# Ones-tile products in two groups (25 and 5), a sixth VectorE row in the first modulation block, and square passes of the second token block's statistics placed later

## The chip, the core and the metric

The kernel runs on one core of one Trainium2 chip. A core has engines that each work through their own list of instructions: TensorE (PE in the profile, with its weight loads as PEld), VectorE (DVE), ScalarE (ACT), GpSimd (POOL) and SyncE (SP), which here issues most DMA transfers. They wait for each other through semaphores. On-chip memory is SBUF; matmul results go to eight PSUM banks of 128 x 512 fp32. The metric is device time of one launch in microseconds (us), smaller is better.

## The reference

One decoder layer on x (4096 tokens x 1024), conditioned by one vector c. `layer_norm` is over the last axis, without affine parameters.

```python
mod = jax.nn.silu(c) @ w_ada + b_ada
shift, scale, gate = jnp.split(mod, 3, axis=-1)
h = layer_norm(x) * (1.0 + scale[:, None, :]) + shift[:, None, :]
proj = h @ w_in + b_in
u_a, z_a, glu_b, z_b = proj[..., :o1], proj[..., o1:o2], proj[..., o2:o3], proj[..., o3:]
pooled = causal_multiscale_pool(u_a)              # windows 2, 4, 8, 16, less the token itself
y_a = jnp.einsum("bsgc,gcd->bsgd", pooled, w_pool) + b_pool
y_a = y_a.reshape(y_a.shape[0], y_a.shape[1], D_POOL) * ls_pool * jax.nn.silu(z_a)
v = glu_b[..., :D_CONV] * jax.nn.sigmoid(glu_b[..., D_CONV:])
v = causal_depthwise_conv(v, w_dw, b_dw)          # 31 taps, 512 channels
v = jax.nn.silu(layer_norm(v) * ln_conv_g + ln_conv_b)
y_b = (v @ w_pw + b_pw) * jax.nn.silu(z_b)
y = jnp.concatenate([y_a, y_b], axis=-1) @ w_out + b_out
x = layer_norm(DEEPNORM_ALPHA * x + gate[:, None, :] * y) * ln_post_g + ln_post_b
```

## The kernel before

**Tiling.** The 4096 tokens are eight blocks of 512 (`NSB`, `T`), each of four tiles of 128 tokens (`TT`); the 1024 features are eight chunks of 128 (`KT`). For the projections a block lies turned, features on the partitions, tokens along the row. Each fp32 operand is split into a high part that TensorE takes as fp32r and a low remainder, and a product of two is three matmuls: high times high (L370), high weight times low x (L371), low weight times high x (L372). `W[n]` are the 20 column groups of `w_in`; groups 8 to 15 (weights `wg0` to `wg7`, one tile for each feature chunk) feed the GLU, 16 and 17 the first half of `z_b` (weights `wz0`, `wz1`).

**Start: modulation and the first block, chunk by chunk.** `c` and the vectors are loaded and turned by small PE transposes (`cps`, `vpsa`). Then PE runs `WARM` = 18 products of a 128 x 128 tile of ones into a bank of their own; nothing reads them. Shift and scale come in five blocks of feature chunks (`mods`). A block's sum over the eight rows k of `w_ada` is divided: the first `MOD_ROWS[b]` rows are added up on DVE (`macc`, L195, or on ACT for the first row of the wide blocks), the others are PE products with a one-column operand (L209), and a last product with the ones tile adds up DVE's share over the partitions. `MOD_SPREAD` deals DVE's rows of the later blocks over the chunks of the first token block. That block is loaded token-wise, normalised (`stats_dve`, ACT), turned on PE (`turn_x`), and `mod_turned` applies scale and shift: ACT writes the high part (L354) and `hs` (L356), DVE the low part. For each chunk k, PE runs six banks (column groups 8, 12, 9, 13, 10, 14) through three groups of six products (L493, then L497, then L501), with the next chunk's transposes between. Four of the banks are of the ring `acc`, two of the ring `s2`; transposes and modulation use the ring `tp` of two. The upper quarter of `wg` comes late, in two loads `w3r` (`w3_cols`, L458), after chunks 5 and 6.

**Statistics of the second block.** Its four token-wise tiles `x_early` are loaded with the last `w_ada` tiles. `col_stats` takes a sum pass over a tile on ACT (L293), the mean on DVE (L294), a square pass on ACT (L298), the variance on DVE (L299) and the reciprocal root on POOL (L300). When all four tiles are done, `to_rows` turns the eight columns on PE, ACT copies them out (`rowsx`, L306), a DMA writes them to DRAM (`rD`) and another reads them back spread over all partitions (`xbc`, L317).

**Later blocks.** `norm_T` loads two turned chunks of x (`xk`, L324), adds the mean (L325) and multiplies by scale and root (L327) on DVE; `mod_xT` adds the shift on ACT and forms the low part on DVE (L337). Column groups 8 to 15 of a block (`glus`) give the banks `p`; `glu` takes a sigmoid on ACT (`sg`, L521) and one DVE pass (`v`, L523), stored to DRAM (`vD`, L524). `z_half` is two more banks (`p1z`). From the third block on statistics are taken in the same way, without early tiles. A second pass then reloads the turned blocks for groups 0 to 7 and the pooling mixer. Beside all of it DVE computes the depthwise convolution (`conv`: loads `cv`, taps L663 and L665, results `ca`), whose results PE turns (L77) for their layer norm. The last stage is the pointwise product, the output projection (`po`, L802) and the post norm.

**What sets the order.** Three engines follow a hand-written order at the start: `seq(engine, inst)` ties an instruction behind the last one that `seq` placed on that engine (`tails[engine]`), without a semaphore. Everything else is placed by the scheduler of the framework, which simulates a timeline and, on each engine, takes what is ready first, by the order of the program. For the statistics of the second block `leads` holds, for each of its four tiles, the tails of ACT and DVE as they stand after chunk 4, 4, 5 and 6: a tile's sum pass and mean come behind them, its square pass and variance wherever the scheduler puts them.

Of the kernel before, what the change touches and what calls it, by code (L numbers as in the profile page):

```python
# [12 lines left out]
AF = mybir.ActivationFunctionType  # L13
ALU = mybir.AluOpType
# [15 lines left out]
WINDOWS = (2, 4, 8, 16)  # L30
UH = 8
EPS = 1e-5
MOD_ROWS = (5, 6, 7, 8, 8)
MOD_SPREAD = ((2, 7), (0, 6), (1, 3), (0, 4), (0, 3), (0, 3))
BLOCKS = ((0, 1), (1, 2), (3, 2), (5, 1))
EARLY = 2
WARM = 18
GATE_SB = 2
PERSB = (1, 1, 1, 1, 1, 1, 0, 0)
ALPHA = 2.0 ** 0.25  # L40
# [3 lines left out]
def tile_layer(ctx, tc, x, x_t, w_in_t, c, w_ada, b_ada, w_in, b_in, w_pool, b_pool, ls_pool, w_dw, b_dw,  # L44
# [81 lines left out]
        nc.vector.tensor_copy(cols[:, c0 : c0 + r0], vps[:, :r0])  # L126

    load_cols((("b_ada", b_ada, 24), ("b_in", b_in, 20)), nc.scalar.dma_start, "a")
    warm = tp_bank("warm")
    for _ in range(WARM):  # L130
        seq("pe", nc.tensor.matmul(warm[:, :P], ones, ones, start=True, stop=True))
# [159 lines left out]
    def col_stats(src, n, nmean, rstd, name, lead=None):  # L291
        sm = st.tile([P, 3], F32, tag=f"sm{name[0]}", bufs=4, name=f"sm{name}")
        i = nc.scalar.activation(src, src, AF.Identity, accum_out=sm[:, 0:1])  # L293
        mean = nc.vector.tensor_scalar(nmean, sm[:, 0:1], -1.0 / n, None, op0=ALU.mult)  # L294
        if lead is not None:
            after(i, lead[0])
            after(mean, lead[1])
        nc.scalar.activation(src, src, AF.Square, bias=nmean, accum_out=sm[:, 1:2])  # L298
        nc.vector.tensor_scalar(sm[:, 2:3], sm[:, 1:2], 1.0 / n, EPS, op0=ALU.mult, op1=ALU.add)  # L299
        nc.gpsimd.tensor_tensor(rstd, sm[:, 2:3], mhalf[:, 0:1], op=ALU.pow)  # L300

    def to_rows(pb, cs, dst, name):
# [6 lines left out]
    def row_stats(sb):  # L309
        cs = st.tile([P, 8], F32, tag="cs", bufs=2, name=f"xcs{sb}")  # L310
        for t in range(TT):
            i = sb * TT + t
            xt = x_early[t] if sb == 1 else load_x(i, t % 2)
            col_stats(xt, D, cs[:, t : t + 1], cs[:, 4 + t : 5 + t], f"x{i}", leads[t] if sb == 1 else None)
        to_rows(tp_bank(f"xcp{sb}"), cs, rD[sb], f"x{sb}")
        bc = ph.tile([P, 2, T], F32, tag="tm", bufs=5, name=f"xbc{sb}")
        nc.sync.dma_start(bc, rD[sb].rearrange("(a t) p -> a (t p)", a=2).partition_broadcast(P))  # L317
        return bc
# [165 lines left out]
    for k in range(KT):  # L484
        lo = both(Wg[k][1])[:, :, : 3 * P]
        seq("dve", nc.vector.tensor_tensor(lo, rows[k], whi.bitcast(F32), op=ALU.subtract))
        sums(k, 0)
        xT.append(mod_turned(pb, k))
        sums(k, 1)
        if k + 1 < KT:  # L490
            whi = cast_w(k + 1)
        for n0, ps in zip(first, pss0):
            seq("pe", nc.tensor.matmul(ps, W[n0][k][0], xT[k][0], start=k == 0, stop=False))  # L493
        if k + 1 < KT:
            pb = turn_x(xt_next, k + 1)
        for n0, ps in zip(first, pss0):
            seq("pe", nc.tensor.matmul(ps, W[n0][k][0], xT[k][1], start=False, stop=False))  # L497
        if k + 1 in starts:
            closers[starts[k + 1]]()
        for n0, ps in zip(first, pss0):  # L500
            seq("pe", nc.tensor.matmul(ps, W[n0][k][1], xT[k][0], start=False, stop=k == KT - 1))  # L501
# [393 lines left out]
```

## Time and profile before

| | |
|---|---|
| median of 3 runs | 1384.91 us (1384.74 to 1386.92) |
| profiled execution, its own time | 1383.35 us |
| its span, first to last instruction | 1381.4 us |
| mean granted TensorE clock | 0.993 |
| HBM read, written | 156.65 MB, 86.04 MB |
| DMA | 243.83 MB, mean 177 GB/s |

The page's second part cuts the span into 40 slices of 34.5 us and gives the busy share of each in tenths, with the clock that the throttle granted to TensorE:

```
PE   7999999999999999999999999999999999999997
DVE  5769999999999889999869998668796999997754
PEclk8999999999999999999999999999999999999999
```

The start is the first two slices. A timeline row names start, length, engine, source line, operation, written tile <- read tiles, their shapes and how many instructions the row holds; brackets give the idle time before it and what ended it. `SPq` is SP's DMA issue, and a `DMA` row is the transfer itself. Tile names in the trace stand without their numbers, so `xk` is `xk_0`, `xk_2` and so on. One product of the program can be several records of PE.

### The profile page before, as it was taken

What the parts mean: (1) busy time and instruction counts of PE and PEld (TensorE: products, weight loads), DVE (VectorE), ACT (ScalarE), POOL (GpSimd) and SP (SyncE); (2) the same over time, 40 slices, a digit from 0 to 9 for tenths busy, and PEclk for the clock granted to TensorE, in tenths of its full rate; (3) what the DMA queues carried; (4) which work ended last, traced back from release to release, by engine and by line L of the source; (5) the groups of instructions that cost most, each with busy time, mean ns of one, the idle gap of its engine ahead of it and who ended that gap; (6) DMA issues with size and microseconds to landing.
All of it is one profiled execution on the core that took longest, in us unless ns stands there. A gap on an engine that the chain in (4) does not pass through costs nothing.

```text
span 1381.4 us, 17276 instructions
## 1 busy us (share of the span) xinstructions
PE 1361.7 (99%) x6109; PEld 1124.7 (81%) x6109; DVE 1188.5 (86%) x2339; ACT 434.1 (31%) x775; POOL 139.4 (10%) x193
## 2 busy tenths in 40 slices
PE   7999999999999999999999999999999999999997
PEld 6788888888888888888888888888888888888886
DVE  5769999999999889999869998668796999997754
ACT  3745654532322341111321123323224131223310
POOL 1001110100000221011110120000111111102101
PEclk8999999999999999999999999999999999999999
DMA  9797857565375586052461535435334434334511
GB/s 313 238 343 274 290 215 271 201 236 198 126 263 191 190 251 218 35 184 76 154 205 64 168 123 191 168 115 177 143 130 158 146 131 161 124 128 135 185 61 76
DMA packets 116552, 243.83 MB, mean 177 GB/s; under 512 B 15154, under 2 KB 49778, under 8 KB 116466
## 3 DMA queue, kind: packets, MB, share of 16 engines
q1 hardware_dynamic: 107184, 209.15, 43.7%
q0 software_dynamic: 9216, 33.56, 7.3%
q8 instruction: 48, 0.79, 0.2%
q14 instruction: 38, 0.31, 0.1%
q10 hardware_dynamic: 66, 0.02, 0.0%
HBM read 156.65 MB, written 86.04 MB: 176 GB/s over the span
## 4 chain that ended last, share of the span: by engine, by line
PE 82%; DVE 9%; DMA 5%; ACT 1%; issue 1%; SPq 1%; DVEq 0%; ACTq 0%
PE po L802 25%; PE p L370 4%; PE p L371 4%; PE p2z L370 4%; PE p2z L371 4%; PE p2u L372 4%; PE p2u L371 4%; PE p2z L372 4%; PE p2u L370 4%; PE p L372 4%; DVE ca L665 2%; PE pw L780 2%; PE pw L779 2%; PE pw L778 2%; PE p2b L371 2%; PE p2b L372 2%
## 5 line engine op out<-in xcount | busy, mean ns | idle before, releaser
L665 DVE SCALAR_TENSOR_TENSOR cx<-cv,wdw,cx 128x257 f32<-128x257 f32 (+1 forms) x240 | 143.0, 607 | 0.2
L665 DVE SCALAR_TENSOR_TENSOR ca<-cx,wsum,ca 128x256 f32<-128x256 f32 (+1 forms) x240 | 142.3, 607 | 0.0
L665 DVE SCALAR_TENSOR_TENSOR ca<-cv,wdw,ca 128x256 f32<-128x256 f32 (+1 forms) x224 | 133.2, 607 | 0.0
L831 POOL TENSOR_TENSOR ors<-ove,mhalf 128x1 f32<-128x1 f32 x32 | 47.9, 1497 | 421.8 <-DVE ove L827 413.4
L825 ACT ACTIVATE ojk<-r,osm 128x1024 bf16<-128x1024 f32 x31 | 35.7, 1151 | 151.5 <-DVE osm L822 151.5
L365 POOL DMA_DIRECT2D x2r<-xD x64 | 34.5, 539 | 467.9 <-PE p2b L372 287.0
L820 DVE SCALAR_TENSOR_TENSOR r<-po,r 128x512 f32<-128x512 f32 x62 | 40.7, 682 | 30.6 <-PE po L802 30.6
L665 DVE SCALAR_TENSOR_TENSOR lx<-lv,wdw,lx 128x257 f32<-128x257 f32 x120 | 57.3, 477 | 0.0
L665 DVE SCALAR_TENSOR_TENSOR la<-lx,wsum,la 128x256 f32<-128x256 f32 x120 | 57.1, 476 | 0.0
L665 DVE SCALAR_TENSOR_TENSOR la<-lv,wdw,la 128x256 f32<-128x256 f32 x112 | 52.5, 477 | 0.1
L300 POOL TENSOR_TENSOR xcs<-smx,mhalf 128x1 f32<-128x1 f32 x28 | 24.0, 859 | 239.1 <-DVE smx L299 206.4
L293 ACT ACTIVATE x<-x 128x1024 f32<-128x1024 f32 x28 | 29.6, 1058 | 57.4 <-DMA x<-in_x_dram 57.1
L336 ACT ACTIVATE x<-xk,shc 128x512 fp32r<-128x512 f32 x56 | 38.0, 721 | 25.3 <-DVE xk L327 23.1
L595 ACT ACTIVATE sz<-p2z,cols 128x512 f32<-128x512 f32 x32 | 22.0, 687 | 73.3 <-PE p2z L372 69.0
L834 DVE SCALAR_TENSOR_TENSOR r<-r,ors,b_bc 128x1024 f32<-128x1024 f32 (+1 forms) x33 | 41.0, 1244 | 2.7 <-POOL ors L831 2.6
L337 DVE SCALAR_TENSOR_TENSOR x<-xk,shc,x 128x512 fp32r<-128x512 f32 x56 | 40.6, 740 | 2.4 <-ACT x L336 2.4
L794 DVE SCALAR_TENSOR_TENSOR r<-r,gbo 128x1024 f32<-128x1024 f32 x32 | 38.9, 1215 | 3.7 <-DMA r<-in_x_dram 3.7
L759 ACT ACTIVATE t<-t,cols 128x512 f32<-128x512 f32 x32 | 23.1, 724 | 60.1 <-DMA t<-tD 52.1
L219 ACT CAST yb<-z 128x512 fp32r<-128x512 f32 x32 | 19.8, 617 | 68.4 <-DVE z L785 58.4
L802 PE MATMUL po<-wo1h,ya 128*128 128x512 f32 x128 | 41.1, 391 | 0.0
L802 PE MATMUL po<-wo0h,ya 128*128 128x512 f32 x128 | 41.0, 390 | 0.0
L602 ACT ACTIVATE u<-p2u,bu 128x512 f32<-128x512 f32 x32 | 22.0, 687 | 59.0 <-PE p2u L372 58.9
(429 smaller groups left out, 4129.7 us busy)
## 6 DMA issues: line engine op xcount, KB each, us to landing
x2r<-xD POOLq DMA_DIRECT2D x64, 512.0 KB, 7.3
xD<-x SPq DMA_DIRECT2D x56, 512.0 KB
x<-in_x_dram SPq DMA_DIRECT2D x32, 512.0 KB
r<-in_x_dram SPq DMA_DIRECT2D x32, 512.0 KB
out_dram<-r SPq DMA_DIRECT2D x31, 512.0 KB
xk<-in_x_t_dram SPq DMA_DIRECT2D x28, 512.0 KB
wa<-in_w_ada_dram SPq DMA_DIRECT2D x32, 256.0 KB
vD<-v SPq DMA_DIRECT2D x32, 256.0 KB
```

What stands on the lines that cost most here:

```text
L336: nc.scalar.activation(h2[:, 0, :], z, AF.Identity, bias=shc[:, k : k + 1])
L337: nc.vector.scalar_tensor_tensor(h2[:, 1, :], z, shc[:, k : k + 1], h2[:, 0, :].bitcast(F32), op0=ALU.add, op1=ALU.subtract)
L370: nc.tensor.matmul(ps, w[0], X[0], start=first, stop=False)
L371: nc.tensor.matmul(ps, w[0], X[1], start=False, stop=False)
L372: nc.tensor.matmul(ps, w[1], X[0], start=False, stop=last)
L665: nc.vector.scalar_tensor_tensor(dst, src, wt, dst, op0=ALU.mult, op1=ALU.add)
L794: xg = nc.vector.scalar_tensor_tensor(r, r, ALPHA, gbo, op0=ALU.mult, op1=ALU.add)
L802: mm = nc.tensor.matmul(po[h], lhs, Wo[k][wi][:, h * 512 : (h + 1) * 512], start=(k == 0 and wi == 0 and lhs is yh), stop=last)
L820: nc.vector.scalar_tensor_tensor(r[:, sl], po[h], 1.0, r[:, sl], op0=ALU.mult, op1=ALU.add, accum_out=sm[:, h : h + 1])
L825: nc.scalar.activation(jk, r, AF.Square, bias=sm[:, 2:3], accum_out=ss)
L831: nc.gpsimd.tensor_tensor(rs, ve, mhalf[:, 0:1], op=ALU.pow)
L834: nc.vector.scalar_tensor_tensor(r[:, sl], r[:, sl], rs, b_bc[:, sl], op0=ALU.mult, op1=ALU.add)
```

## The change

It edits four places:

- `MOD_ROWS[0]` goes from 5 to 6: in the first modulation block DVE adds up six rows and PE multiplies two, in place of five and three.
- The 18 products of the ones tile become a function `keep_warm(i)`, which writes to a bank of the ring `s2` in place of `tp`. It is called for 25 products at the old place and for 5 more behind the transposes of chunk 0 (`turn_x(xt_next, 0)`), ahead of that chunk's first products.
- `leads` becomes `ends`, the tails of ACT and DVE after every chunk. `X_STATS` names two chunks for each tile of the second block: sum pass and mean go behind the first one's tails (4, 4, 5, 6, as before), square pass and variance now behind the second one's (5, 7, 7, 7).
- In `col_stats` the four instructions of sum and square are tied in one loop.

From the second edit on all lines move down: what was L293, L298, L306, L317, L324, L325, L337, L370, L521 and L665 is L297, L299, L310, L321, L328, L329, L341, L374, L526 and L670.

```diff
@@ -30,11 +30,12 @@
 WINDOWS = (2, 4, 8, 16)
 UH = 8
 EPS = 1e-5
-MOD_ROWS = (5, 6, 7, 8, 8)
+MOD_ROWS = (6, 6, 7, 8, 8)
 MOD_SPREAD = ((2, 7), (0, 6), (1, 3), (0, 4), (0, 3), (0, 3))
 BLOCKS = ((0, 1), (1, 2), (3, 2), (5, 1))
 EARLY = 2
-WARM = 18
+X_STATS = ((4, 5), (4, 7), (5, 7), (6, 7))
+WARM = (25, 5)
 GATE_SB = 2
 PERSB = (1, 1, 1, 1, 1, 1, 0, 0)
 ALPHA = 2.0 ** 0.25
@@ -126,9 +127,12 @@
         nc.vector.tensor_copy(cols[:, c0 : c0 + r0], vps[:, :r0])
 
     load_cols((("b_ada", b_ada, 24), ("b_in", b_in, 20)), nc.scalar.dma_start, "a")
-    warm = tp_bank("warm")
-    for _ in range(WARM):
-        seq("pe", nc.tensor.matmul(warm[:, :P], ones, ones, start=True, stop=True))
+    def keep_warm(i):
+        ps = s2_bank(f"warm{i}")
+        for _ in range(WARM[i]):
+            seq("pe", nc.tensor.matmul(ps[:, :P], ones, ones, start=True, stop=True))
+
+    keep_warm(0)
     wdw = cst.tile([P, CW * MC], F32, name="wdw")
     wsum = cst.tile([P, HQ + 1, MC], F32, name="wsum")
     wd3 = wdw.rearrange("p (j m) -> p j m", m=MC)
@@ -292,11 +296,11 @@
         sm = st.tile([P, 3], F32, tag=f"sm{name[0]}", bufs=4, name=f"sm{name}")
         i = nc.scalar.activation(src, src, AF.Identity, accum_out=sm[:, 0:1])
         mean = nc.vector.tensor_scalar(nmean, sm[:, 0:1], -1.0 / n, None, op0=ALU.mult)
+        sq = nc.scalar.activation(src, src, AF.Square, bias=nmean, accum_out=sm[:, 1:2])
+        var = nc.vector.tensor_scalar(sm[:, 2:3], sm[:, 1:2], 1.0 / n, EPS, op0=ALU.mult, op1=ALU.add)
         if lead is not None:
-            after(i, lead[0])
-            after(mean, lead[1])
-        nc.scalar.activation(src, src, AF.Square, bias=nmean, accum_out=sm[:, 1:2])
-        nc.vector.tensor_scalar(sm[:, 2:3], sm[:, 1:2], 1.0 / n, EPS, op0=ALU.mult, op1=ALU.add)
+            for inst, (act, dve), eng in ((i, lead[0], 0), (mean, lead[0], 1), (sq, lead[1], 0), (var, lead[1], 1)):
+                after(inst, (act, dve)[eng])
         nc.gpsimd.tensor_tensor(rstd, sm[:, 2:3], mhalf[:, 0:1], op=ALU.pow)
 
     def to_rows(pb, cs, dst, name):
@@ -311,7 +315,7 @@
         for t in range(TT):
             i = sb * TT + t
             xt = x_early[t] if sb == 1 else load_x(i, t % 2)
-            col_stats(xt, D, cs[:, t : t + 1], cs[:, 4 + t : 5 + t], f"x{i}", leads[t] if sb == 1 else None)
+            col_stats(xt, D, cs[:, t : t + 1], cs[:, 4 + t : 5 + t], f"x{i}", [ends[k] for k in X_STATS[t]] if sb == 1 else None)
         to_rows(tp_bank(f"xcp{sb}"), cs, rD[sb], f"x{sb}")
         bc = ph.tile([P, 2, T], F32, tag="tm", bufs=5, name=f"xbc{sb}")
         nc.sync.dma_start(bc, rD[sb].rearrange("(a t) p -> a (t p)", a=2).partition_broadcast(P))
@@ -447,7 +451,7 @@
     first = (8, 12, 9, 13, 10, 14)
     pss0 = [acc_bank(f"p1_0_{n0}") for n0 in first[:4]] + [s2_bank(f"p1_0_{n0}") for n0 in first[4:]]
     starts = {k0: b for b, (k0, nk) in enumerate(mods)}
-    leads = []
+    ends = []
 
     def w3_cols(q):
         raw = wraw(f"w3r{q}").rearrange("p (k h c) -> p k h c", k=4, h=2)
@@ -475,6 +479,7 @@
     closers[0]()
     whi = cast_w(0)
     pb = turn_x(xt_next, 0)
+    keep_warm(1)
 
     def sums(k, part):
         if k < len(MOD_SPREAD):
@@ -499,7 +504,7 @@
             closers[starts[k + 1]]()
         for n0, ps in zip(first, pss0):
             seq("pe", nc.tensor.matmul(ps, W[n0][k][1], xT[k][0], start=False, stop=k == KT - 1))
-        leads += [(tails["act"], tails["dve"])] * (0, 0, 0, 0, 2, 1, 1, 0)[k]
+        ends.append((tails["act"], tails["dve"]))
         if k in (5, 6):
             w3_cols(k - 5)
     assert not steps
```

The scheduler's order follows these ties, and it moves more than the four places name. In the rows below, numbers behind a tile's name are the framework's count (`x_446` and `x_449` are the second block's token-wise tiles), and a row's end is the shape.

**ACT, end of the first block** (chunk 7 to the first `sg`). Before, `x_446` is the last of the four tiles (the square passes of the other three stand further ahead, `x_444` two rows ahead of it), `hs_7` the last step of the chunk, and `x_1096` a tile of the third block:

```order
L298 ACTIVATE x_446,smx_888<-x_446,xcs_869 128x1024
L356 ACTIVATE hs_7_792<-x_0_7_790,shn 128x512
L219 CAST wz0h<-wzr_857 128x1024
L219 CAST wz1h<-wzr_863 128x1024
L306 COPY rowsx_896<-xcp_894 8x128
L521 ACTIVATE sg_0_911<-p_0_12_453,cols 128x512
L521 ACTIVATE sg_1_916<-p_0_13_455,cols 128x512
L521 ACTIVATE sg_2_921<-p_0_14_457,cols 128x512
L293 ACTIVATE x_1096,smx_1098<-x_1096 128x1024
```

The same stretch of the change:

```order
L360 ACTIVATE hs_7_804<-x_0_7_802,shn 128x512
L223 CAST wz0h<-wzr_869 128x1024
L299 ACTIVATE x_449,smx_888<-x_449,xcs_881 128x1024
L299 ACTIVATE x_451,smx_894<-x_451,xcs_881 128x1024
L299 ACTIVATE x_453,smx_900<-x_453,xcs_881 128x1024
L223 CAST wz1h<-wzr_875 128x1024
L526 ACTIVATE sg_0_923<-p_0_12_460,cols 128x512
L526 ACTIVATE sg_1_928<-p_0_13_462,cols 128x512
L297 ACTIVATE x_1108,smx_1110<-x_1108 128x1024
L310 COPY rowsx_908<-xcp_906 8x128
L526 ACTIVATE sg_2_933<-p_0_14_464,cols 128x512
```

Three square passes have gone from ahead of `hs_7` to between the two casts of `wz`, and `rowsx` has gone from ahead of the first sigmoid to behind the second and a sum pass of the third block.

**SP's queue, same place.** It issues the statistics' way through DRAM (`rD`, `xbc`), the `xk` loads, the third block's tiles (`x_...<-in_x_dram`) and the GLU's stores (`vD`). Before:

```order
L307 DMA rD_289<-rowsx_896 8x128
L288 DMA x_1096<-in_x_dram 128x1024
L288 DMA x_1104<-in_x_dram 128x1024
L317 DMA xbc_899<-rD_289 128x1024
L324 DMA xk_0_901<-in_x_t_dram 128x2x512
L324 DMA xk_2_906<-in_x_t_dram 128x2x512
L524 DMA vD_0_184<-v_0_913 128x512
```

And of the change, where `cv_0` is the first load of the convolution:

```order
L292 DMA x_1116<-in_x_dram 128x1024
L529 DMA vD_0_191<-v_0_925 128x512
L311 DMA rD_296<-rowsx_908 8x128
L529 DMA vD_0_199<-v_1_930 128x512
L292 DMA x_1124<-in_x_dram 128x1024
L659 DMA cv_0_6493<-vD_0_191 128x2x256
L321 DMA xbc_911<-rD_296 128x1024
L328 DMA xk_0_913<-in_x_t_dram 128x2x512
L328 DMA xk_2_918<-in_x_t_dram 128x2x512
```

Two GLU stores, the third tile of the third block and `cv_0` now stand ahead of `xbc`.

**DVE, norm of the second block**, from the first pass over `xk_0` to the low part of its first chunk, `x_1_0`. Before:

```order
L325 TENSOR_TENSOR xk_0_901<-xk_0_901,xbc_899 128x1024
L299 TENSOR_SCALAR smx_1106<-smx_1106 128x1
L327 SCALAR_TENSOR_TENSOR xk_0_901<-xk_0_901,s_300,xbc_899 128x512 x2
L325 TENSOR_TENSOR xk_2_906<-xk_2_906,xbc_899 128x1024
L523 SCALAR_TENSOR_TENSOR v_2_923<-p_0_10_456,cols,sg_2_921 128x512
L337 SCALAR_TENSOR_TENSOR x_1_0_981<-xk_0_901,shc,x_1_0_981 128x512
```

Of the change, from two rows behind its first pass over `xk_0` (twelve more rows, taps of the convolution and statistics of the third block, stand right ahead of that pass) to the same row:

```order
L670 SCALAR_TENSOR_TENSOR ca_0_6494<-cv_0_6493,wdw,ca_0_6494 128x256
L670 SCALAR_TENSOR_TENSOR ca_0_6494<-cx_0_6495,wsum,ca_0_6494 128x256
L329 TENSOR_TENSOR xk_2_918<-xk_2_918,xbc_911 128x1024
L528 SCALAR_TENSOR_TENSOR v_3_990<-p_0_11_938,cols,sg_3_988 128x512
L331 SCALAR_TENSOR_TENSOR xk_0_913<-xk_0_913,s_307,xbc_911 128x512 x2
L670 SCALAR_TENSOR_TENSOR cx_0_6495<-cv_0_6493,wdw,cx_0_6495 128x257
L670 SCALAR_TENSOR_TENSOR ca_0_6494<-cv_0_6493,wdw,ca_0_6494 128x256
L670 SCALAR_TENSOR_TENSOR ca_0_6494<-cx_0_6495,wsum,ca_0_6494 128x256
L329 TENSOR_TENSOR xk_4_1009<-xk_4_1009,xbc_911 128x1024
L331 SCALAR_TENSOR_TENSOR xk_2_918<-xk_2_918,s_307,xbc_911 128x512 x2
L329 TENSOR_TENSOR xk_6_1014<-xk_6_1014,xbc_911 128x1024
L341 SCALAR_TENSOR_TENSOR x_1_0_993<-xk_0_913,shc,x_1_0_993 128x512
```

Taps of the convolution and the passes over `xk_2`, `xk_4` and `xk_6` now stand between the first pass over `xk_0` and `x_1_0`; on PE the second block's first products wait for `x_1_0`, and begin with three high ones (`p_1_8`, `p_1_12`, `p_1_9`, L374) where one stood before.

## The prediction

> **What bounds the kernel now.** I read the page first, then the chain of waits, then busy time by stretch, then each engine's timeline up to 115 us.
>
> ```profile
> PE 1361.7 (99%) x6109; PEld 1124.7 (81%) x6109; DVE 1188.5 (86%) x2339; ACT 434.1 (31%) x775; POOL 139.4 (10%) x193
> PE 82%; DVE 9%; DMA 5%; ACT 1%; issue 1%; SPq 1%; DVEq 0%; ACTq 0%
> 100.00:160.00 60.00, 60.00 (x267) 49.50 (x266) 54.59 (x133) 32.20 (x53) 7.01 (x8) 1.00 0.79 292
> 260.00:360.00 100.00, 100.00 (x462) 83.12 (x462) 98.47 (x159) 36.10 (x60) 5.88 (x7) 1.00 0.57 204
> ```
>
> The first two rows are engine busy times and the shares of the chain; the other two are stretches (length, then PE, PEld, DVE, ACT, POOL busy, then the granted clock). PE is the bound: from 70 us on it has no gap worth naming, so the end is the moment at which PE's unbroken run begins plus a fixed amount of products. A microsecond won or lost before 70 us, or a new hole in the run, moves the end one for one. DVE is close behind (54.59 of 60 us), so a change in DVE's order can open such a hole.
>
> ```profile
> 0.84 0.17 DVE L70 MEMSET ones<- 128x128 f32 x1 [0.84 <-PEq L878]
> 5.82 6.92 PE L131 MATMUL warm<-ones 128*128 128x128 f32 x36
> 14.29 0.96 PE L209 MATMUL mod<-sc,wa 128*128 128x1 f32 x6 [1.55 <-DMA wa<-in_w_ada_dram]
> 13.84 1.01 DVE L195 SCALAR_TENSOR_TENSOR macc<-wa,sc,macc 128x256 f32<-128x256 f32 x2
> 19.21 2.93 PE L493 MATMUL p<-x,wg0h 128*128 128x512 f32 x6 [0.87 <-ACT x L354]
> 35.52 2.76 PE L493 MATMUL p<-x,wg2h 128*128 128x512 f32 x6
> 41.60 1.53 PE L493 MATMUL p<-x,wg3h 128*128 128x512 f32 x6
> 15.00:18.00 3.00, 3.00 (x16) 2.94 (x15) 0.54 (x4) 1.48 (x2) 0.00 (x0) 0.50 1.18 305
> 36.00:38.00 2.00, 2.00 (x6) 1.50 (x5) 1.97 (x4) 0.69 (x1) 0.00 (x0) 0.50 1.10 347
> 57.00:60.00 3.00, 1.15 (x6) 0.61 (x5) 2.40 (x9) 2.97 (x7) 0.55 (x1) 1.00 0.01 3
> ```
>
> Timeline rows read start, length, engine, line, output<-input, count, and in brackets the wait before and its releaser. The granted clock is 0.50 in 15 to 18 us and again in 36 to 38: six products take 2.76 us there and 1.53 at full clock.
>
> **The products and the sixth row: no effect on the end.** Two records make one product, so 18 products take 6.92 us, 0.38 each. Twenty-five take 9.6 us; from 1.0 us, when `ones` is set, with two small transposes between, they are over near 11.2, and the wait for w_ada still ends at 14.29. The gap ahead of it grows from 1.55 to about 3 us, and after 1.55 the clock was already at 0.50, so I expect it there again. In the first modulation block PE loses two of eight products (four records of 0.16 us, 0.64 us) and DVE gains one row of 0.5 us, which the first summing product then waits for by some 0.3: net 0.3 us earlier. The five products take 1.9 us where PE waited 0.87: up to 1.0 us later. An unbroken run may lift the clock sooner, and six half-clock products cost 1.2 us more. So PE reaches the second modulation block between 1.5 us earlier and 1 us later. What hides it:
>
> ```profile
> 53.67 0.41 ACT L458 CAST wg0h<-w3r 128x256 fp32r<-128x256 f32 x1 [0.73 <-DMA w3r<-in_w_in_dram]
> 57.45 1.13 ACT L298 ACTIVATE x<-x,xcs 128x1024 f32<-128x1024 f32 x1
> 58.58 0.76 ACT L354 ACTIVATE x<-xt,shc,s 128x512 fp32r<-128x512 f32 x1
> 59.39 1.68 PE L493 MATMUL p<-x,wg6h 128*128 128x512 f32 x6 [1.85 <-ACT x L354]
> 65.93 0.71 ACT L356 ACTIVATE hs<-x,shn 128x512 f32<-128x512 f32 x1
> 66.54 1.03 ACT L219 CAST wz0h<-wzr 128x1024 fp32r<-128x1024 f32 x1
> 68.89 0.25 ACT L306 COPY rowsx<-xcp 8x128 f32<-8x128 f32 x1
> 69.63 1.27 ACT L521 ACTIVATE sg<-p,cols 128x512 f32<-128x512 f32 x2 [0.49 <-PE p L501]
> 70.37 0.50 PE L370 MATMUL p<-x,wg0h 128*128 128x512 f32 x1
> ```
>
> At 59.39 PE has waited 1.85 us for ACT, and ACT's work there hangs on a load that lands at 53.67 whatever PE did. A gain before lengthens that wait, a loss of under 1.85 us shortens it. I take 0; were the cover gone, the ends above would count in full.
>
> **The square passes: PE's run begins 1.2 us earlier.** After the casts at 53.67 ACT ran one sum and two squares (1.13 us each) ahead of chunk 6; now one, so chunk 6 starts 1.13 us earlier, near 58.3. Of the four squares, three stood ahead of `hs_7` after 57 us; 3 x 1.13 = 3.4 us off 66.54 lets ACT be done with `hs_7` at 63.1. PE then has the block's last product done near 67.7 instead of 70.37. But ACT now runs the first cast of wz (0.95 us), three squares (3.4), the second cast (0.96) and `sg_0` (0.64) in a row: 69.1. `p_0_11`, the first product of the unbroken run, needs the bank that `sg_0` reads (before, too, it followed it by 0.1). So it starts at 69.2 against 70.37: 1.2 us gained, between 0.5 and 1.6, as casts and loads fall. The transpose of the statistics needs the last square, 67.5, plus about 1 us over DVE and POOL: earlier than 69.2.
>
> **The statistics' way to the second block: late.** `rowsx`, the copy that sends the statistics on, now stands behind `sg_0`, `sg_1` and a sum pass for the third block: 69.7 plus 1.14 plus 0.2 is 71.05, against 69.14.
>
> ```profile
> 69.82 0.33 SPq L307 DMA_DIRECT2D rD<-rowsx  x1
> 73.35 0.33 SPq L317 DMA_DIRECT2D xbc<-rD  x1
> 73.72 0.94 SPq L324 DMA_DIRECT2D xk<-in_x_t_dram  x2
> 76.43 1.06 ACT L293 ACTIVATE x<-x 128x1024 f32<-128x1024 f32 x1 [3.31 <-DMA x<-in_x_dram]
> 97.27 7.36 DMA cv<-vD
> 81.25 1.23 DVE L325 TENSOR_TENSOR xk<-xk,xbc 128x1024 f32<-128x1024 f32 x1 [0.97 <-DMA xk<-in_x_t_dram]
> 82.51 1.41 DVE L327 SCALAR_TENSOR_TENSOR xk<-xk,s,xbc 128x512 f32<-128x512 f32 x2
> 83.84 1.22 DVE L325 TENSOR_TENSOR xk<-xk,xbc 128x1024 f32<-128x1024 f32 x1
> 84.98 0.74 DVE L523 SCALAR_TENSOR_TENSOR v<-p,cols,sg 128x512 f32<-128x512 f32 x1
> 85.64 1.40 DVE L337 SCALAR_TENSOR_TENSOR x<-xk,shc,x 128x512 fp32r<-128x512 f32 x2
> 105.01 0.35 DVE L663 TENSOR_SCALAR cx<-cv,wdw 128x257 f32<-128x257 f32 x1
> 111.28 0.88 DVE L665 SCALAR_TENSOR_TENSOR cx<-cv,wdw,cx 128x257 f32<-128x257 f32 x2
> 92.49 0.39 PE L371 MATMUL p<-x,wg0h 128*128 128x512 f32 x1
> ```
>
> On SP's queue `xbc` now also stands behind a load of x for the third block, which must wait until ACT has squared the tile before it (near 72.9), and behind `cv_0`, a read of what the glu wrote only at 70.3. `rD` to `xbc` took 3.5 us before; I put `xbc` at 75.2 and the two `xk` loads at 75.6, 1.9 us later than 73.72. By the same 7.5 us to landing, `xk_0` would be there at 83.1.
>
> On DVE twelve conv and statistics rows stand ahead of `xk_0`: four first passes of about 0.27 us, six of 0.40 and two or three small ones, 3.7 us from the landing of `cv_0`. That takes at most the 7.36 us of the chain's row, from 74.6 at most to 82, and the norm then starts at 85.7; with an earlier landing nothing is lost beyond the data. I take 83.5; the ends are 81.25 (as before) and 85.7. From there to `x_1_0` DVE had 5.1 us of work (81.25 to 86.3). Now six conv rows (2.4 us), two more first passes over xk_4 and xk_6 (2.3) and the scaling of xk_2 (1.3) stand in it: 11.0 us, so `x_1_0` is there at 94.5. PE wants its low half at 92.49 less the 1.2 won, plus two high products that now go first (0.46): 91.75. **A hole of 2.8 us**, with ends of 0.5 and 5.0. The later chunks follow DVE at under 2 us each while PE now spends 2.7 on each, so they add nothing.
>
> **The clock after the hole.** A wait of 1.55 us ahead of 14.29 left the clock at 0.50, one of 1.85 us ahead of 59.39 left it at 1.00. For 2.8 us I expect one piece of half clock like that of 36 to 38 us: six products at 2.76 instead of 1.53, a transpose group with them, 1.5 us; the ends are 0 and 1.7.
>
> The Trainium skill, page "TensorE: Matmul & The Clock Gate", table "Why this matters for your kernels", asks only that gaps between bursts stay under about 3 us, and its section on the HAM clock gate drops the clock after one idle window of about 3.4 us. By that rule the hole costs no clock, and it speaks against this change's first 25 products, whose end lies about that far ahead of 14.29. By that rule the sum below would end 1.5 us earlier. This trace disagrees in one place (0.50 after 1.55 us of wait) and agrees in the other (1.00 after 1.85).
>
> **The sum**, on the profiled execution's 1383.35 us (span 1381.4 and 1.95 around it): 1.2 off, 2.8 on, 1.5 on, +3.1, so 1386.45. The median shown, 1384.91, stands 1.56 above that execution; the same for the change gives **1388.0 us**, 0.22% slower. About 0.2%, 2.8 us, is what a measurement of this kernel can tell from no change, so 1387.7 is the edge.
>
> **Rivals.**
> - *The hole without the clock loss.* For it speaks 59.39. It gives 1388.0 less 1.5, 1386.5. Chance 0.20.
> - *No hole: the conv rows fill a wait that DVE has anyway.* DVE stood idle ahead of 81.25, waiting for `xk`. If the norm starts by 80.75, `x_1_0` is there when PE wants it. That needs `xbc` and `cv_0` landing no later than `xbc` did before. Then only the early gain stays: 1384.9 less 1.2, 1383.7, not slower. Chance 0.18.
> - *DVE falls further behind.* The order moves conv work of later blocks too, and DVE's margin is thin:
>
> ```profile
> 231.45 0.48 DVE L675 SCALAR_TENSOR_TENSOR ca<-cx,cols,ca 128x256 f32<-128x256 f32 x1
> 232.19 0.38 PE L77 MATMUL cl<-ident,ca 128*128 128x128 f32 x2
> ```
>
>   A transpose follows its conv result by 0.26 us here. With the hole at its upper end of 5.0 us and 1 us at such a place the time is 1384.9 + 6.3 = 1391.2. Against it: conv work done earlier gives later transposes more room. Chance 0.17.
> - *The change does what its words say*, and the clock is full from the modulation on, and w3r's casts come earlier with it. Only with PE's run also starting another 2 us sooner and no hole is it below 1382.1. Chance 0.05.
>
> **How the numbers follow.** The forecast itself has 0.40, with times from 1386.9 to 1389.5; 0.26 of that lies above 1387.7. Slower: 0.26, all 0.17 of the third rival and 0.02 of the first, 0.45. Faster: 0.05 and 0.02 of the second, 0.07. Within: 0.48. The range runs from 1383.4, just under the no-hole time, to 1391.5, just over the third rival.
>
> **What would show it.** Right: clock 0.50 after 14.3 us; chunk 6 on PE near 58.3; `p_0_11` near 69.2 after a wait for `sg_0`; DVE's first pass over `xk_0` near 83.5 with conv rows ahead of it; a PE wait of about 3 us near 92 put down to DVE's L341, and the clock below 1.00 behind it; no PE wait later. Wrong: `xk_0` started before 81, or PE unbroken through 92; then I have overrated the queue on SP. A PE wait at a conv transpose would show the third rival.

## The result, and the profile after

| | before | change |
|---|---|---|
| median of 11 runs, us | 1386.1 (1382.92 to 1391.35) | 1395.9 (1388.54 to 1398.91) |
| ratio, 95% interval | | 1.0059 (1.0039 to 1.0079) |
| profiled execution, us | 1383.35 | 1388.54 |
| its span, mean granted clock | 1381.4, 0.993 | 1386.4, 0.990 |

The change is slower by 0.6%. The median lies above the range of the prediction, and the single runs show how: two of the eleven are at 1388.5 and 1389.1, close above the forecast of 1388.0, and nine at 1392.9 to 1398.9. One execution of run 6 (4494.56 us) and one of run 7 (1708.33) are left out of the ratios below. The first trace is of the fastest run. It is read first, since it tests the steps of the prediction; the second group comes with the experiments.

From the page of the change, engine busy times and the chain's shares by engine:

```profile
PE 1365.6 (99%) x6129; PEld 1127.8 (81%) x6129; DVE 1189.8 (86%) x2340; ACT 438.5 (32%) x777; POOL 136.9 (10%) x193
...
PE 90%; DVE 4%; DMA 4%; SPq 1%; issue 0%; ACT 0%; DVEq 0%; ACTq 0%
```

PE is busy 3.9 us longer, and the span has grown by 5.0. Most of the 3.9 is no loss: the 30 products of ones take 10.55 us where the 18 took 6.92, in time in which PE had waited. What the change loses is waits and a lower clock later on. What PE waited for in the change (total us, times, longest):

```profile
PE mod L213 <- DMA wa<-in_w_ada_dram: 4.3, 1, 4.3
PE p L375 <- DVE x L341: 2.8, 1, 2.8
PE xcp L78 <- POOL xcs L304: 1.4, 1, 1.4
...
PE cl L78 <- DVE ca L680: 1.1, 1, 1.1
...
PE p L498 <- ACT x L358: 0.7, 1, 0.7
```

The timeline of PE, at the places that the prediction named:

```profile
58.68 1.66 PE L498 MATMUL p<-x,wg6h 128*128 128x512 f32 x6 [0.74 <-ACT x L358]
...
69.56 0.27 PE L78 MATMUL xcp<-ident,xcs 128*8 128x128 f32 x1 [1.40 <-POOL xcs L304]
69.73 0.50 PE L374 MATMUL p<-x,wg0h 128*128 128x512 f32 x1
...
91.67 1.26 PE L374 MATMUL p<-x,wg0h 128*128 128x512 f32 x3
95.78 0.50 PE L375 MATMUL p<-x,wg0h 128*128 128x512 f32 x1 [2.85 <-DVE x L341]
```

Chunk 6 starts at 58.68 (59.39 before), the unbroken run at 69.73 (70.37 before), and behind three high products it breaks for 2.85 us: this pause is called the hole below. The other engines on the way to that hole, from the timeline of the same execution (start and duration in us, engine, line, operation, what it waited for in brackets), ACT first, then SP, then DVE:

```profile
54.93 0.41 ACT L462 CAST wg2h<-w3r 128x256 fp32r<-128x256 f32 x1 [0.51 <-DMA w3r<-in_w_in_dram]
...
69.00 1.25 ACT L526 ACTIVATE sg<-p,cols 128x512 f32<-128x512 f32 x2
...
71.20 0.24 ACT L310 COPY rowsx<-xcp 8x128 f32<-8x128 f32 x1
...
76.78 0.61 SPq L659 DMA_DIRECT2D cv<-vD  x1
77.48 0.54 SPq L321 DMA_DIRECT2D xbc<-rD  x1
...
80.16 0.44 DVE L664 TENSOR_TENSOR cx<-cv 128x271 f32<-128x271 f32 x1 [0.96 <-DMA cv<-vD]
...
84.74 1.23 DVE L329 TENSOR_TENSOR xk<-xk,xbc 128x1024 f32<-128x1024 f32 x1 [0.85 <-DMA xk<-in_x_t_dram]
...
93.84 1.22 DVE L329 TENSOR_TENSOR xk<-xk,xbc 128x1024 f32<-128x1024 f32 x1
94.98 0.75 DVE L341 SCALAR_TENSOR_TENSOR x<-xk,shc,x 128x512 fp32r<-128x512 f32 x1
```

`rowsx` comes 2.3 us later than before. `xbc` stands on SP behind `cv_0`, ahead of which SP waits 3.2 us until the GLU's store has landed. The norm starts at 84.74 (81.25 before), and DVE does taps and three more passes before `x_1_0`, whose low part is done at 95.73. The clock behind the hole, in stretches of 2 us (length, PE, PEld, DVE, ACT, POOL busy, granted clock, DMA share, GB/s):

```profile
96.00:98.00 2.00, 2.00 (x8) 1.59 (x8) 2.00 (x5) 0.00 (x0) 0.00 (x0) 0.78 1.06 407
98.00:100.00 2.00, 2.00 (x7) 1.54 (x6) 2.00 (x4) 1.38 (x2) 0.00 (x0) 0.50 1.25 345
100.00:102.00 2.00, 2.00 (x9) 1.66 (x8) 2.00 (x5) 1.07 (x2) 0.00 (x0) 0.87 0.77 209
```

A clock of 0.78, 0.50 and 0.87 over 2 us each is 3.4 us of half clock (0.88 + 2 + 0.52): 1.7 us lost. In this execution the sum is 0.64 off, 2.85 and 1.7 on, and 1.13 on for a wait at a convolution's transpose near 763, less 0.38 for such a wait near 259 in the kernel before: 4.7 of the 5.0 us.

### The profile page after: what moved, and what is told of

It reads as the page before. It is cut to its first block, busy times and chain, and to the rows that moved or that the text cites. A ratio compares the mean times of both kernels' runs of the same rounds, so it can differ in the third digit from the quotient of the medians.

```text
span 1386.4 us, 17312 instructions
## 1 busy us (share of the span) xinstructions
PE 1365.6 (99%) x6129; PEld 1127.8 (81%) x6129; DVE 1189.8 (86%) x2340; ACT 438.5 (32%) x777; POOL 136.9 (10%) x193
## 4 chain that ended last, share of the span: by engine, by line
PE 90%; DVE 4%; DMA 4%; SPq 1%; issue 0%; ACT 0%; DVEq 0%; ACTq 0%
PE po L807 25%; PE p L375 7%; PE p L374 7%; PE p L376 7%; PE p2z L374 4%; PE p2z L375 4%; PE p2z L376 4%; PE p2u L374 4%; PE p2u L375 4%; PE p2u L376 4%; PE pw L785 2%; PE pw L784 2%; PE pw L783 2%; PE p1z L376 2%; PE p1z L375 2%; PE p1z L374 2%
## 5 line engine op out<-in xcount | busy, mean ns | idle before, releaser
L670 DVE SCALAR_TENSOR_TENSOR ca<-cx,wsum,ca 128x256 f32<-128x256 f32 (+1 forms) x240 | 146.3, 612 | 0.0
L670 DVE SCALAR_TENSOR_TENSOR cx<-cv,wdw,cx 128x257 f32<-128x257 f32 (+1 forms) x240 | 145.0, 615 | 0.3
L670 DVE SCALAR_TENSOR_TENSOR ca<-cv,wdw,ca 128x256 f32<-128x256 f32 (+1 forms) x224 | 136.6, 612 | 0.0
L670 DVE SCALAR_TENSOR_TENSOR lx<-lv,wdw,lx 128x257 f32<-128x257 f32 x120 | 57.0, 475 | 0.0
L670 DVE SCALAR_TENSOR_TENSOR la<-lx,wsum,la 128x256 f32<-128x256 f32 x120 | 56.8, 473 | 0.0
L670 DVE SCALAR_TENSOR_TENSOR la<-lv,wdw,la 128x256 f32<-128x256 f32 x112 | 53.1, 474 | 0.2
L304 POOL TENSOR_TENSOR ccs<-smc,mhalf 128x1 f32<-128x1 f32 x32 | 31.0, 975 | 135.1 <-DVE smc L300 134.9
L304 POOL TENSOR_TENSOR xcs<-smx,mhalf 128x1 f32<-128x1 f32 x28 | 19.4, 693 | 248.8 <-DVE smx L300 200.0
L341 DVE SCALAR_TENSOR_TENSOR x<-xk,shc,x 128x512 fp32r<-128x512 f32 x56 | 40.6, 745 | 0.8 <-ACT x L340 0.8
L526 ACT ACTIVATE sg<-p,cols 128x512 f32<-128x512 f32 x32 | 21.8, 686 | 58.3 <-PE p L376 39.2
L807 PE MATMUL po<-wo3h,ya 128*128 128x512 f32 x128 | 40.3, 389 | 0.0
```

Of the source, the lines that this page charges most:

```text
L341: nc.vector.scalar_tensor_tensor(h2[:, 1, :], z, shc[:, k : k + 1], h2[:, 0, :].bitcast(F32), op0=ALU.add, op1=ALU.subtract)
L670: nc.vector.scalar_tensor_tensor(dst, src, wt, dst, op0=ALU.mult, op1=ALU.add)
L807: mm = nc.tensor.matmul(po[h], lhs, Wo[k][wi][:, h * 512 : (h + 1) * 512], start=(k == 0 and wi == 0 and lhs is yh), stop=last)
```

## The experiments

Each kernel ran 12 times beside 35 runs of the kernel before on the same chip, in three batches (1 to 4, 5 to 8, 9 to 12). Times are medians.

**1. The start alone** (`MOD_ROWS` and the products, statistics as before; below it, 8 is the same kernel).

```diff
-MOD_ROWS = (5, 6, 7, 8, 8)
+MOD_ROWS = (6, 6, 7, 8, 8)
-WARM = 18
+WARM = (25, 5)
```

> Only the first two edits: 25 and 5 products of the ones tile and the sixth row on VectorE; statistics placed as before. Theory A (the start is hidden by ScalarE's wait ahead of chunk 6): ratio 1.000 within 0.002, chunk 6 on PE again near 59.4. Rival B (the start pays: clock lost ahead of the first modulation or products in the way): 2 us or more slower, ratio above 1.0015, and chunk 6 later than 60.

Measured: ratio 1.0022 (1.0005 to 1.0039), 1388.23 us; chunk 6 at 59.98, `p_0_11` at 71.53, 1.2 us later than before. PE waited 2.36 us ahead of chunk 5 and 2.48 ahead of chunk 6, and each time 3.4 us of half clock followed. The ratio is above rival B's 1.0015, but chunk 6 is not later than 60: that speaks for B, weakly.

**2. The square passes alone** (`X_STATS`, with 18 products and five rows).

```diff
-MOD_ROWS = (6, 6, 7, 8, 8)
-WARM = (25, 5)
+MOD_ROWS = (5, 6, 7, 8, 8)
+WARM = 18
...
-    keep_warm(1)
```

> Only the later square passes, with 18 products and five rows as before. Theory A (all of the loss comes from the order that the scheduler makes of these ties): the time of the whole change, ratio 1.006 within 0.002; a PE wait of 2 to 4 us for DVE's low part of x_1_0 near 92 and some 3.4 us of half clock behind it. Rival B: at least 2 us nearer to the kernel before.

Measured: 1.0034 (1.0014 to 1.0054), 1390.56 us, beside 1.0043 for the whole change in the same batch: below the 1.004 to 1.008 expected, but not 2 us below the change. PE waits 2.85 us near 96 with 6.8 us of half clock about it: theory A for the place. But the traced execution took 1395.02, and a larger loss lay elsewhere: 4.74 us, with half clock behind, at a transpose of convolution statistics.

**3. The change once more.**

> The changed kernel once more, for the trace of another execution; the first trace was of the fastest of 11. Theory A1 (the start's hole is much the same each time, and the rest above 1388.5 us is lost where PE waits for convolution results, a place that differs from execution to execution): the hole near 92 is 2.3 to 3.5 us and the waits for ca add up to the rest. Rival A2 (the hole near 92 itself swings with how late the statistics' transfers land): the hole is 2.9 us plus what the execution lies above 1388.5.

Measured: 1.0043 (1.0022 to 1.0063); six runs from 1386.65 to 1389.50, six from 1393.88 to 1397.99, none between. The trace is of the upper group (1394.33). The hole near 96 is 2.86 us, as in the first trace, behind a wait of 0.93 for ACT's `sgz`, and it ends at the same time (95.76): A2 falls. The waits for `ca` are 0.7: A1 falls too. The rest is here. The waits of PE in run 3 (total us, times, longest):

```profile
PE ccp L78 <- POOL ccs L304: 4.6, 1, 4.6
```

Its timeline about that place, POOL, DVE, PE, DVE:

```profile
830.55 10.56 POOL L304 TENSOR_TENSOR ccs<-smc,mhalf 128x1 f32<-128x1 f32 x2 [0.61 <-DVE smc L300]
...
840.22 0.48 DVE L670 SCALAR_TENSOR_TENSOR la<-lx,wsum,la 128x256 f32<-128x256 f32 x1
...
841.17 0.38 PE L78 MATMUL ccp<-ident,ccs 128*8 128x128 f32 x1 [4.64 <-POOL ccs L304]
...
845.73 0.43 DVE L619 TENSOR_TENSOR us<-u 128x256 f32<-128x256 f32 x1 [5.03 <-ACT u L607]
```

And the stretch of 3.5 us behind it (columns as above):

```profile
841.00:844.50 3.50, 3.33 (x9) 2.65 (x10) 0.00 (x0) 0.25 (x1) 0.11 (x1) 0.52 0.08 16
```

`ccs` is the last step of convolution block 5's statistics: POOL takes a reciprocal root of 128x1, called the root below. Two of them stand in POOL's row, 10.56 us; the second alone took 9.85. It ended at 841.11, and DVE's unbroken run of taps had ended at 840.70. DVE stopped only because it needed `u`, which ACT makes from a product of PE, and PE stood behind `ccp`, waiting for POOL. Ahead of `ccp` PE lost 4.64 us, and of 3.4 us of half clock 3.2 fell behind it and cost another 1.6: 6.2 us. The two traced executions of the change differ by 5.8, which is 6.2 less 0.5 for a shorter wait near 763. The groups lie 7.0 apart (medians of all 23 runs of the change: eight at 1388.9, fifteen at 1395.9); only one of the fifteen was traced. In run 2 the root took 9.85 us too and ended 0.41 us after the last tap, as here.

Before, the same root found DVE standing (timeline of the kernel before, DVE, POOL, DVE):

```profile
829.27 0.16 DVE L299 TENSOR_SCALAR smc<-smc 128x1 f32<-128x1 f32 x1
...
829.51 0.55 POOL L300 TENSOR_TENSOR ccs<-smc,mhalf 128x1 f32<-128x1 f32 x1 [0.39 <-DVE smc L299]
...
833.01 0.35 DVE L663 TENSOR_SCALAR la<-lv,wdw 128x256 f32<-128x256 f32 x1 [3.58 <-DMA lv<-vD]
```

The order had changed there: in the kernel before, the row behind the last variance waits for a load of `lv`; in the change 24 rows of one operation with two tile inputs stand in its place. VectorE's order of the change, cut after six:

```
L300 TENSOR_SCALAR smc_3_7746<-smc_3_7746 128x1
L670 SCALAR_TENSOR_TENSOR la_2_8381<-lv_2_8382,wdw,la_2_8381 128x256
L670 SCALAR_TENSOR_TENSOR lx_1_7831<-lv_1_7830,wdw,lx_1_7831 128x257
L670 SCALAR_TENSOR_TENSOR la_0_7773<-lv_1_7830,wdw,la_0_7773 128x256
L631 SCALAR_TENSOR_TENSOR pp_3_5760<-pp_3_5760,bpl,sz_3_5719 128x512
L670 SCALAR_TENSOR_TENSOR la_0_7773<-lx_1_7831,wsum,la_0_7773 128x256
```

The new theory: **POOL's root is starved by DVE's run of two-input passes, and whether it slips in first is decided by small shifts.** In the first trace it did. Both roots stand in POOL's row of that execution:

```profile
831.71 1.43 POOL L304 TENSOR_TENSOR ccs<-smc,mhalf 128x1 f32<-128x1 f32 x2
```

They took 0.66 and 0.80 us, beside the same unbroken passes of DVE, and each ended some 0.4 us after the end of one of them. So the run alone does not shut POOL out each time. Of 1344 such roots in the 14 traces 787 took at most 1 us and seven over 2.5. What decides at which pass end POOL gets in is not shown; small shifts are a guess.

**4. The convolution held back:** block 0's loads `cv` behind the `xk` loads on SP, its first row on DVE behind the low part of `x_1_3` (`HOLD` = 3).

```diff
+            ld = nc.sync.dma_start(v[:, :, HQ + i * TH : HQ + (i + 1) * TH], vD[m][s0 + i])
+            if s0 == 0:
+                after(ld, x_loads[1])
...
+        i = nc.vector.tensor_tensor(sm, od[:, : N + HQ], ev[:, 1 : N + HQ + 1], op=ALU.add)
+        if s0 == 0:
+            after(i, lows[1, HOLD])
```

> The whole change, and the first convolution block tied behind the second block's norm: its loads cv behind the xk loads on SP, its first DVE row behind the low part of x_1_3. Theory A: xbc is issued near 74 (77.5 in the change), the norm starts near 81.5, x_1_0 is done near 87, PE has no hole near 92 and no half clock behind it, 4.5 us less than the change: 1384 us where the change has 1388.5. Theory A2: the whole loss goes, ratio 1.000 or less. Theory A1: 3 to 6 us of waits for ca stay in the timed runs, ratio 1.002 to 1.004. Rival C (DVE is simply short of time and what isn't done at 92 is missing later): the ratio stays at 1.005 or more, the time lost at waits for ca between 150 and 300.

Measured: 0.9987 (0.9972 to 1.0002), 1383.49 us. From its timeline, SP's `xbc`, then DVE's first pass over `xk_0` and the low parts of `x_1_0` and `x_1_1`:

```profile
75.90 0.32 SPq L322 DMA_DIRECT2D xbc<-rD  x1
...
83.14 1.23 DVE L331 TENSOR_TENSOR xk<-xk,xbc 128x1024 f32<-128x1024 f32 x1 [1.01 <-DMA xk<-in_x_t_dram]
...
87.53 1.41 DVE L343 SCALAR_TENSOR_TENSOR x<-xk,shc,x 128x512 fp32r<-128x512 f32 x2
```

PE and its clock through the place of the hole, in run 4 (length, PE, PEld, DVE, ACT, POOL busy, clock, DMA share, GB/s):

```profile
92.00:100.00 8.00, 8.00 (x37) 6.64 (x36) 7.16 (x11) 3.51 (x6) 0.00 (x0) 1.00 1.05 395
```

`xbc` goes out 1.6 us earlier than in the change, not 3.5 as expected, but `x_1_0` is done near 88.3 and the hole is gone: theory A for the place. The ratio is that of A2, and rival C falls. (The traced execution, 1388.29, is one of the two longest of the twelve: PE waits 3.37 us at a convolution's transpose near 490.) This order also has a shorter run behind the last variance (12 two-input passes, and both roots took 0.7 us), so both losses are gone at once.

**5. The starved root cured.** DVE copies the root, so that it has to wait for POOL there.

```diff
-        nc.gpsimd.tensor_tensor(rstd, sm[:, 2:3], mhalf[:, 0:1], op=ALU.pow)
+        gate = name.startswith("c5")
+        nc.gpsimd.tensor_tensor(sm[:, 0:1] if gate else rstd, sm[:, 2:3], mhalf[:, 0:1], op=ALU.pow)
+        if gate:
+            nc.vector.tensor_copy(rstd, sm[:, 0:1])
```

> The whole change; the reciprocal root of convolution block 5 goes from POOL to a free column of smc, and a 128x1 copy on VectorE takes it to ccs, so that VectorE waits for POOL there instead of running 24 taps past it. Nothing is left out. Theory S (in the long executions POOL's last root waits 9.85 us for a pause in VectorE's taps and PE waits 4.6 us for it near 837, with 3.4 us of half clock behind): no PE wait for ccp over 1 us, the last root under 2 us, the group of runs 5 to 7 us above the others is gone, median 1388 to 1389.5, ratio 1.001 to 1.003, no run above 1392. Rival T (the upper group has another cause, as transfers that land late): half of the runs stay 5 us or more above the lowest, ratio 1.004 or more.

Measured: 1.0024 (1.0011 to 1.0037), 1389.39 us; eleven runs from 1386.59 to 1390.81 and one at 1392.99, above the 1392 expected; no wait for `ccp`. From the timeline of run 5, both roots on POOL, then DVE's last tap ahead of the copies and the second copy:

```profile
832.13 4.21 POOL L305 TENSOR_TENSOR smc<-smc,mhalf 128x1 f32<-128x1 f32 x2 [0.94 <-DVE smc L300]
...
835.45 0.48 DVE L673 SCALAR_TENSOR_TENSOR la<-lv,wdw,la 128x256 f32<-128x256 f32 x1
...
836.38 0.15 DVE L307 COPY ccs<-smc 128x1 f32<-128x1 f32 x1 [0.38 <-POOL smc L305]
```

The second root was starved again (3.50 us, not the under 2 expected) and ended at 836.34, 0.41 us after the last tap. But now DVE stops at its copy, before PE needs the result, and the group near 1396 is gone: theory S, and rival T falls.

**6. The convolution held back on DVE alone** (`cv_0` stays ahead of `xbc` on SP; all three first passes are tied). Against run 4:

```diff
-            if s0 == 0:
-                after(ld, x_loads[1])
...
+                i = nc.vector.tensor_scalar(dst, src, wt, None, op0=ALU.mult)
+                if s0 == 0:
+                    after(i, lows[1, HOLD])
```

> As the run with the convolution held back, but only on VectorE: cv_0 stays ahead of xbc on SP, the first taps come behind the low part of x_1_3. Theory D (the hole near 92 comes from the convolution's rows between xk_0 and x_1_0): xbc is issued near 77.5 as in the change, the norm starts near 84, x_1_0 is done near 89.5 and PE, which wants it at 91.9, has no wait there. Rival Q (the queue on SP is enough by itself): a hole of 1 us or more stays near 92. In time: 1384 in an execution without other waits by D, 1386 or more by Q.

Measured: 1.0038 (1.0026 to 1.0050), 1391.38 us. The norm, from DVE's timeline in run 6:

```profile
83.57 1.23 DVE L331 TENSOR_TENSOR xk<-xk,xbc 128x1024 f32<-128x1024 f32 x1 [2.36 <-DMA xk<-in_x_t_dram]
...
87.96 1.40 DVE L343 SCALAR_TENSOR_TENSOR x<-xk,shc,x 128x512 fp32r<-128x512 f32 x2
```

PE's longest wait there, from the waits:

```profile
PE cl L79 <- DVE ca L686: 6.9, 1, 6.9
```

And a stretch about its end, at 764.07:

```profile
761.00:768.00 7.00, 3.93 (x11) 3.17 (x12) 6.83 (x19) 1.00 (x3) 0.00 (x0) 0.51 0.16 40
```

Theory D holds for the hole near 92: with `cv_0` ahead on SP (`xbc` at 76.64), `x_1_0` is still done at 88.7 and PE doesn't wait. The time, above Q's 1386, speaks for neither, because this tie made another order downstream, in which PE waits 6.9 us for a convolution result at 764 and has 6.8 us of half clock, 4.0 of them after the wait: the prediction's third rival, in a kernel that is not the change. Less these 8.9 us the traced execution (1390.61) would be at 1381.7, an estimate from these rows.

**7. Both cures** (4 and 5 together), and **10**, the same once more.

> The whole change with both cures: the first convolution block behind the second block's norm on SP and VectorE, and VectorE's copy of the root in convolution block 5. Nothing is left out. If hole and starved root are all that the change loses: ratio 0.9985 or less, median 1383 or less, no run above 1387. If something else is left: the ratio of the run with the convolution held back, 0.9987, or more.

Measured: 0.9984 (0.9969 to 0.9999), 1384.44 us.

> The whole change with both cures once more, on the same chip as the run with the old start: ratio 0.998 to 0.999 by either theory; the difference to the old start is what is asked.

Measured: 0.9987 (0.9971 to 1.0004), 1384.04 us. The traces have no wait near 92 and none at `ccp` over 0.3 us. But the median of 7 is above the 1383 expected and two more of its runs lie above 1387, and run 4, without the copy, had the same 0.9987: the copy adds nothing to that order. With hole and starved root gone the change's loss is gone, and the medians of runs 4, 7 and 10 (1383.5 to 1384.4) are within 0.8 us of the prediction's time without a hole, 1383.7; that nothing else is lost is not shown.

**8. The start alone, again.**

> The products and the sixth row alone, once more: the first time gave 1.0022 with an interval from 1.0005 to 1.0039. Theory A (hidden by the wait ahead of chunk 6): 1.000 within 0.0015. Theory B2 (PE comes to chunks 5 and 6 earlier, waits longer there, and pays for it with half clock behind the waits): ratio 1.0015 to 1.003; waits over 2 us ahead of chunk 5 or 6, half clock between 50 and 64, and p_0_11 after 71.

Measured: 1.0018 (1.0000 to 1.0035), 1388.96 us, in the range of B2; but `p_0_11` is at 70.64, not after 71, with a wait of 3.45 us ahead of chunk 6 with no half clock behind it, and one of 2.66 us at a convolution transpose near 617.

**9. Both cures with the old start.** Against run 7:

```diff
-MOD_ROWS = (6, 6, 7, 8, 8)
-WARM = (25, 5)
+MOD_ROWS = (5, 6, 7, 8, 8)
+WARM = 18
```

> Later square passes with both cures (first convolution block behind the second block's norm, root copied on VectorE), and the start as before: 18 products, five rows. Nothing is left out. Theory B3 (the 30 products and the sixth row cost some 2.5 us by themselves, as in two runs of the start alone): ratio 0.995 to 0.9975, 2 us or more under the same kernel with the new start. Theory A (the start is hidden): within 1 us of the same kernel with the new start, ratio near 0.9985.

Measured: 0.9984 (0.9969 to 0.9998), 1383.92 us, 0.1 us from 10 in the same batch. In this order the start costs nothing: theory A, B3 falls.

**11. The products alone**, five rows kept.

> The kernel before with 25 and 5 products in place of 18, five rows kept. If the products are what costs: ratio 1.0015 to 1.0025, as with the sixth row. If it is the row (VectorE has one row more ahead of the first modulation): 1.000 within 0.001. If the start costs nothing: 1.000 too.

Measured: 1.0006 (0.9985 to 1.0027): it decides nothing. The traced run was the longest of the twelve (1396.0), with 5.28 us of PE waiting at 623.

**12. The kernel before, again.**

> The kernel before, unchanged, for the trace of another execution: what a ratio of the same kernel to itself gives here (1.000 within 0.0015), where p_0_11 starts (70.4 in the first trace; 70.2 to 70.8 if the start repeats), and whether PE waits for convolution results in it (0.4 us in the first trace; 1 to 5 us in executions of the median and above).

Measured: 0.9994 (0.9979 to 1.0009); `p_0_11` at 70.78, no wait for a convolution result over 0.2 us. The traced execution (1383.39) lies below the median, so what the longer executions of the kernel before wait for was not seen.

So the start by itself is not settled: 1.0022 and 1.0018 in the kernel before, nothing in the cured one. The three traces with the new products and the old order of the statistics (1, 8, 11) have one thing in common that both traces of before lack, a wait near 617 to 623. The issues of a load `cv` on SP and of the first reload `x2r` on POOL near 595, and DVE's wait for that load, from the timeline of the kernel before:

```profile
592.49 0.58 SPq L652 DMA_DIRECT2D cv<-vD  x1
...
593.68 0.53 POOL L365 DMA_DIRECT2D x2r<-xD  x1 [48.58 <-PE p2b L372]
...
599.26 0.49 DVE L663 TENSOR_SCALAR cx<-cv,wdw 128x513 f32<-128x513 f32 x1 [0.21 <-DMA cv<-vD]
```

The same three from the timeline of run 1:

```profile
595.95 0.53 POOL L368 DMA_DIRECT2D x2r<-xD  x1 [49.11 <-PE p2b L375]
...
596.07 0.58 SPq L656 DMA_DIRECT2D cv<-vD  x1
...
608.01 0.49 DVE L667 TENSOR_SCALAR cx<-cv,wdw 128x513 f32<-128x513 f32 x1 [5.38 <-DMA cv<-vD]
```

Before, `cv` goes out 1.2 us ahead of the first of eight reloads, and DVE waits 0.21 us; in run 1 it goes out 0.12 us behind it, and DVE waits 5.38; in runs 8 and 11 it goes out 0.93 and 1.18 behind, and DVE waits 5.79 and 8.16. No run tested this order by itself. SP waits for DVE's last use of the load's buffer there; why that comes later was not found.

## Why the prediction was wrong, and where it was right

**The products and the row: no effect.** In the traced execution as said: the wait ahead of the first modulation grew (to 4.33 us, not 3), the clock fell to 0.50 there, chunk 0 began at 19.70 (19.21 before), the second modulation 1.15 us earlier than before, and a wait ahead of chunk 6 (0.74 us) still covered the difference. Run 9 against 10 agrees; runs 1 and 8 give 2.5 to 3 us by their ratios, and these stay open.

**The square passes: 1.2 us earlier.** Right in sign; in size 0.64 in the first trace and 1.40 in run 3 (`p_0_11` at 68.97). In the first trace ACT waited 0.51 us at 54.93 for the second `w3r` load, where before its casts ran on, so chunk 6 came 0.7 us earlier as against 1.1, and `sg_0` ended at 69.68 as against 69.1. `p_0_11` followed it by 0.05, as said. PE's last wait before was for POOL's `xcs` (1.40 us), later than the prediction had it, but that transpose started at 69.56, before `sg_0` had ended, so it cost next to nothing.

**The late statistics: a hole of 2.8 us.** Shown: 2.85 to 2.86 us in four traces (the change twice, runs 2 and 5). That the size came out so well is in part luck, since two errors of 1.2 us cancel. `xbc` was 2.3 us later than said (the 3.2 us that SP waits ahead of `cv_0` are not in the prediction), the norm started at 84.7 for 83.5, and the low half was done at 95.7 for 94.5; the 11.0 us of DVE's work between were right. And PE came at 92.9 for 91.75: its run began 0.5 later than said, and the third high product waited for ACT's `sgz`, a wait that the prediction doesn't have. Runs 4 and 6 show which part carries the hole: with `xbc` still late but the taps, and with them the early passes over `xk_2`, `xk_4` and `xk_6`, out of the way of `x_1_0`, it is gone.

**The clock: 1.5 us.** Measured 1.7 in the first trace, one piece of 3.4 us. The Trainium skill, page "TensorE: Matmul & The Clock Gate", table "Why this matters for your kernels", would have had no loss for gaps under about 3 us; the traces here disagree (2.85 us, with half clock behind it, in four of them).

**The sum: +3.1 us.** For the eight runs of the lower group it holds: their median, 1388.9, is 2.8 above the 1386.1 of before. The two profiled executions are 5.2 apart, since less was gained at the start than said (0.64 for 1.2) and 1.13 us were lost near 763.

**What failed is "no PE wait later"**, and with it the chance of 0.17 and the price of 1 us for a later wait. The step behind it took only DVE's results `ca` as what a later transpose can wait for, and argued that early taps give them more room. Room was not the matter. The order downstream had put 24 two-input passes right behind the last variance of block 5, and in run 3 POOL's root of 128x1 ended only when they were through: 6.2 us. Run 5, in which DVE waits for the root, has none of the group that held fifteen of the change's 23 runs. The rows of the new order showed that run before any execution; they were read for how much work DVE has, not for what it shuts out.

The Trainium skill, page "SBUF — State Buffer", section "SBUF: two separate sides", says that a VectorE instruction with two SBUF inputs and a GpSimd one that reads SBUF exclude each other, whichever starts first, for the whole instruction. Most roots here agree: 1270 of the 1344 took at most 1.6 us, which leaves room for about one pass beside their own 0.55. Runs 2 and 3 go further: by one instruction the root would have waited 0.5 us; it waited through 24.

## What to carry to other kernels

When a change lets a scheduler reorder, read the new order for what each waiting engine needs, the small helpers on POOL among it, and not only for the amount of work ahead of it. A tiny POOL operation whose result PE waits for is at risk beside a long run of two-input VectorE passes, even if one trace shows it slipping in: give VectorE an instruction that waits for it, as in run 5. And where a result falls into two groups, trace one run of each before explaining the median.

## What the hardware did that was not expected

- POOL's root of 128x1 takes 0.55 us beside an idle DVE and up to 9.85 beside unbroken two-input passes. In three executions (the change again, runs 2 and 5) it ended 0.41 us after the last of them; in the first trace of the change two took 0.66 and 0.80 beside the same passes.
- In 14 traces, of 28 waits of PE from 0.7 to 1.97 us (after 36 us, ahead of the last product) none was followed by half clock; of 22 from 1.99 to 6.91 us, 21 were, in pieces of 3.4 or 6.8 us. The one that wasn't had 3.45 us. The limit lies near 2 us in these traces; ahead of 36 us, among small modulation products, the clock also fell behind shorter waits (0.50 after 1.55 us in the kernel before).
- A load issued 0.12 us behind the first of eight 512 KB reloads held DVE up for 5.38 us; issued 1.2 us ahead of it, 0.21. The order was not tested by itself.
